# Two neighbouring rows per partition in a batch-norm and ReLU kernel: runs of 8 KB in HBM instead of 4 KB

## The chip, the cores and the metric

The kernel runs on one core of one Trainium2 chip. The metric is the device time of one execution in microseconds.

Some words: HBM is the memory outside the core, SBUF the core's own memory with 128 partitions, and DMA moves data between them. A *run* of bytes is a stretch that is contiguous in memory (an experiment is called a run too, by its label); a *packet* is one record of a DMA engine in the trace; a *queue* is where an engine issues its transfers (sync, scalar or POOL). A *dip* is a stretch in which the transfer rate falls below its *plateau*, the rate in the middle of the kernel.

## The reference

Inference batch norm followed by ReLU on a tensor of 32 images, 128 channels and 32 x 32 pixels in float32: 16.8 MB in, 16.8 MB out, and almost no arithmetic.

```python
# x: (32, 128, 32, 32); gamma, beta, running_mean, running_var: (128,); eps = 1e-5
normalized = (x - running_mean[None, :, None, None]) / np.sqrt(running_var[None, :, None, None] + eps)
scaled = normalized * gamma[None, :, None, None] + beta[None, :, None, None]
return np.maximum(scaled, 0)
```

Gamma and variance are 1, beta and mean are 0. The kernels compute scale and bias from the tables all the same.

## The kernel before

A partition holds one channel. A tile is two images, so the 8 KB that a partition gets come from two places in HBM, 512 KB apart, 4 KB each. Tile 0 and eleven others are loaded from the sync queue, four (1, 3, 5, 7) from the scalar queue, which also issues all stores. The four parameter tables are loaded from POOL, each as one row in one SBUF partition, and four tiny matmuls (eight passes in the trace) turn them into columns.

```python
x3 = x.rearrange("b c h w -> b c (h w)")
...
engine.dma_start(out=t[:, j*step:(j+1)*step],
                 in_=x3[b0 + j*step : b0 + (j+1)*step].transpose([1, 0, 2]))     # 4 KB runs
...
nc.gpsimd.dma_start(out=prow[0:1, 3*C:4*C], in_=running_var[None, :])            # four such rows
...
nc.scalar.activation(out=t[:, :nb], in_=t[:, :nb], func=Relu, bias=bias_t[:, 0:1], scale=scale_t[:, 0:1])
nc.scalar.dma_start(out=out3[b0 : b0 + nb].transpose([1, 0, 2]), in_=t[:, :nb])
```

The first tile is stored in small pieces (256, 768 and 1,024 columns of one image each), so that stores can begin early.

Of the kernel before, what the change touches and what calls it, by code (L numbers as in the profile page):

```python
# [1 line left out]

# [4 lines left out]


@with_exitstack
def kernel(  # L10
    ctx: ExitStack,
    tc: tile.TileContext,
    x: bass.AP,
    gamma: bass.AP,
    beta: bass.AP,
    running_mean: bass.AP,
    running_var: bass.AP,
    eps: bass.AP,
    out: bass.AP,
):  # L20
    nc = tc.nc

    B, C, H, W = x.shape
    HW = H * W
    assert C == nc.NUM_PARTITIONS, f"expected {nc.NUM_PARTITIONS} channels, got {C}"

    x3 = x.rearrange("b c h w -> b c (h w)")
    out3 = out.rearrange("b c h w -> b c (h w)")

    f32 = mybir.dt.float32  # L30

    NBMAX = 2
    n_tiles = B // NBMAX
    sizes = [NBMAX] * n_tiles
    scalar_tiles = (1, 3, 5, 7)
    splits = {0: 2, 1: 2}
    BUFS = 16
    SEPARATE_PSUM = True
    FIRST_PIECES = (256, HW - 256)

    params = ctx.enter_context(tc.tile_pool(name="params", bufs=1))
    eps_t = params.tile([C, 1], f32)
    nc.vector.memset(eps_t, float(eps))  # L43
    prow = params.tile([1, 4 * C], f32)
    one_t = params.tile([1, 1], f32)
    nc.vector.memset(one_t, 1.0)  # L46

    data = ctx.enter_context(tc.tile_pool(name="data", bufs=BUFS))
    tiles = {}
    for i in (0,) + scalar_tiles:  # L50
        tiles[i] = data.tile([C, NBMAX, HW], f32, name="t")

    def emit_input(i, t, engine):
        nsp = splits.get(i, 1)
        step = NBMAX // nsp
        b0 = i * NBMAX
        for j in range(nsp):
            engine.dma_start(  # L58
                out=t[:, j * step : (j + 1) * step],
                in_=x3[b0 + j * step : b0 + (j + 1) * step].transpose([1, 0, 2]),  # L60
            )

    nc.gpsimd.dma_start(out=prow[0:1, 3 * C : 4 * C], in_=running_var[None, :])  # L63
    nc.gpsimd.dma_start(out=prow[0:1, 0 * C : 1 * C], in_=gamma[None, :])  # L64
    nc.gpsimd.dma_start(out=prow[0:1, 2 * C : 3 * C], in_=running_mean[None, :])  # L65
    nc.gpsimd.dma_start(out=prow[0:1, 1 * C : 2 * C], in_=beta[None, :])  # L66

    emit_input(0, tiles[0], nc.sync)
    for i in scalar_tiles:
        emit_input(i, tiles[i], nc.scalar)  # L70

    pp = ctx.enter_context(tc.tile_pool(name="pp", bufs=1, space=bass.MemoryType.PSUM))
    if SEPARATE_PSUM:
        pcols = [pp.tile([C, 1], f32, name=f"p{k}") for k in range(4)]
    else:
        pc = pp.tile([C, 4], f32)
        pcols = [pc[:, k : k + 1] for k in range(4)]
    for k in (3, 0, 2, 1):
        nc.tensor.matmul(  # L79
            pcols[k],  # L80
            prow[0:1, k * C : (k + 1) * C],
            one_t[0:1, 0:1],
            start=True,
            stop=True,
        )
    g_col, b_col, mu_col, var_col = pcols

    std_t = params.tile([C, 1], f32)
    nc.scalar.activation(  # L89
        out=std_t,  # L90
        in_=var_col,
        func=mybir.ActivationFunctionType.Sqrt,
        bias=eps_t[:, 0:1],
        scale=1.0,
    )
    rstd_t = params.tile([C, 1], f32)
    nc.vector.reciprocal(out=rstd_t, in_=std_t)  # L97
    scale_t = params.tile([C, 1], f32)
    nc.vector.tensor_mul(out=scale_t, in0=g_col, in1=rstd_t)  # L99
    ms_t = params.tile([C, 1], f32)  # L100
    nc.vector.tensor_mul(out=ms_t, in0=mu_col, in1=scale_t)  # L101
    bias_t = params.tile([C, 1], f32)
    nc.vector.tensor_sub(out=bias_t, in0=b_col, in1=ms_t)  # L103

    out_ring = {}
    n_out = [0]

    def relu_store(t, b, img, c0, c1):
        nc.scalar.activation(  # L109
            out=t[:, img : img + 1, c0:c1],  # L110
            in_=t[:, img : img + 1, c0:c1],
            func=mybir.ActivationFunctionType.Relu,
            bias=bias_t[:, 0:1],
            scale=scale_t[:, 0:1],
        )
        eng = out_ring.get(n_out[0], nc.scalar)
        n_out[0] += 1
        eng.dma_start(
            out=out3[b : b + 1, :, c0:c1].transpose([1, 0, 2]),
            in_=t[:, img : img + 1, c0:c1],  # L120
        )

    for i, nb in enumerate(sizes):
        b0 = i * NBMAX
        if i in tiles:
            t = tiles.pop(i)
        else:
            t = data.tile([C, NBMAX, HW], f32, name="t")
            emit_input(i, t, nc.sync)
        if i == 0:  # L130
            c0 = 0
            for w in FIRST_PIECES:
                relu_store(t, b0, 0, c0, c0 + w)
                c0 += w
            for img in range(1, nb):
                relu_store(t, b0 + img, img, 0, HW)
        else:
            nc.scalar.activation(  # L138
                out=t[:, :nb],
                in_=t[:, :nb],  # L140
                func=mybir.ActivationFunctionType.Relu,
                bias=bias_t[:, 0:1],
                scale=scale_t[:, 0:1],
            )
            nc.scalar.dma_start(out=out3[b0 : b0 + nb].transpose([1, 0, 2]), in_=t[:, :nb])  # L145


# [1 line left out]
_INS = ['x', 'gamma', 'beta', 'running_mean', 'running_var', 'eps']  # L149
_OUTS = [((32, 128, 32, 32), 'float32')]  # L150
#: Inputs that are plain numbers.
_NUMBERS = {'eps': 1e-05}


# [26 lines left out]
```

## Time and profile before

| what | value |
|---|---|
| time, median | 86.78 us (86.53 to 86.80) when predicted; 86.53 to 86.64 in the rounds of the experiments |
| span of the profiled execution | 84.6 us |
| ScalarE busy, the busiest compute engine | 34.8 us (41%) |
| DMA traffic | 33.57 MB in 9,025 packets |
| plateau of the transfer rate | 419 to 421 GB/s |

The lines are shown in the prediction. The DMA row gives the busy share of the 16 DMA engines by slice of a fortieth of the span (2.1 us), in tenths; the row under it what they moved. In a table of stretches the last two numbers of a row are the DMA share and the rate in GB/s, and the numbers before them are the busy times of the compute engines. A share of about 1 with a low rate means that the DMA engines are busy with slow packets.

### The profile page before, as it was taken

What the parts mean: (1) busy time and instruction counts of PE and PEld (TensorE: products, weight loads), DVE (VectorE), ACT (ScalarE), POOL (GpSimd) and SP (SyncE); (2) the same over time, 40 slices, a digit from 0 to 9 for tenths busy, and PEclk for the clock granted to TensorE, in tenths of its full rate; (3) what the DMA queues carried; (4) which work ended last, traced back from release to release, by engine and by line L of the source; (5) the groups of instructions that cost most, each with busy time, mean ns of one, the idle gap of its engine ahead of it and who ended that gap; (6) DMA issues with size and microseconds to landing.
All of it is one profiled execution on the core that took longest, in us unless ns stands there. A gap on an engine that the chain in (4) does not pass through costs nothing.

```text
span 84.6 us, 153 instructions
## 1 busy us (share of the span) xinstructions
PE 2.3 (3%) x8; PEld 2.0 (2%) x8; DVE 0.7 (1%) x6; ACT 34.8 (41%) x20; POOL 2.3 (3%) x8
## 2 busy tenths in 40 slices
PE   0007300000000000000000000000000000000000
PEld 0006300000000000000000000000000000000000
DVE  0001100000000000000000000000000000000000
ACT  0321479006920791000049598792987910000000
POOL 5500000000000000000000000000000000000000
DMA  1999999999999999999999999999999999999991
GB/s 35 333 411 353 405 420 418 418 409 410 402 416 416 420 420 424 420 422 420 418 426 420 422 420 418 426 416 424 418 422 422 416 426 420 420 420 418 424 422 74
DMA packets 9025, 33.57 MB, mean 397 GB/s; under 512 B 704, under 2 KB 832, under 8 KB 9024
## 3 DMA queue, kind: packets, MB, share of 16 engines
q10 hardware_dynamic: 5616, 20.97, 61.0%
q1 hardware_dynamic: 3280, 12.58, 36.9%
q0 software_dynamic: 128, 0.00, 0.1%
q14 instruction: 1, 0.01, 0.0%
HBM read 16.78 MB, written 16.78 MB: 396 GB/s over the span
## 4 chain that ended last, share of the span: by engine, by line
DMA 65%; ACT 7%; ACTq 4%; issue 3%
DMA t<-in_x_dram 65%; ACT t L138 7%; ACTq L58 2%; ACTq L145 2%
## 5 line engine op out<-in xcount | busy, mean ns | idle before, releaser
L138 ACT ACTIVATE t<-t,bias_t,scale_t 128x2048 f32<-128x2048 f32 x15 | 30.6, 2084 | 24.7 <-DMA t<-in_x_dram 22.3
L109 ACT ACTIVATE t<-t,bias_t,scale_t 128x256 f32<-128x256 f32 (+2 forms) x3 | 2.8, 950 | 2.4 <-DVE bias_t L103 2.0
L89 ACT ACT_TABLE_LOAD x1 | 1.3, 1283 | 3.5 <-issue 3.5
L79 PE MATMUL p<-one_t,prow 1*128 1x1 f32 x8 | 2.3, 354 | 7.2 <-DMA prow<-in_running_var_dram 6.8
L79 PEld LDWEIGHTS p<-one_t,prow 1*128 1x128 f32 x8 | 2.0, 306 | 7.4 <-issue 6.8
L89 ACT ACTIVATE std_t<-p,eps_t 128x1 f32<-128x1 f32 x1 | 0.3, 261 | 2.7 <-PE p L79 2.7
L63 POOL DMA_DIRECT2D prow<-in_running_var_dram x1 | 0.6, 617 | 0.8 <-POOLq L162 0.8
L65 POOL DMA_DIRECT2D prow<-in_running_mean_dram x1 | 0.5, 487 | 0.0
L64 POOL DMA_DIRECT2D prow<-in_gamma_dram x1 | 0.5, 484 | 0.0
L66 POOL DMA_DIRECT2D prow<-in_beta_dram x1 | 0.5, 484 | 0.0
L97 DVE RECIPROCAL rstd_t<-std_t 128x1 f32<-128x1 f32 x1 | 0.2, 164 | 6.8 <-ACT std_t L89 6.8
L103 DVE TENSOR_TENSOR bias_t<-p,ms_t 128x1 f32<-128x1 f32 x1 | 0.2, 158 | 0.6 <-PE p L79 0.6
L99 DVE TENSOR_TENSOR scale_t<-p,rstd_t 128x1 f32<-128x1 f32 x1 | 0.2, 159 | 0.2 <-PE p L79 0.2
L101 DVE TENSOR_TENSOR ms_t<-p,scale_t 128x1 f32<-128x1 f32 x1 | 0.2, 157 | 0.4 <-PE p L79 0.4
L162 POOL MEMSET const-float32-0.0<- 128x1 f32 x1 | 0.1, 98 | 0.2 <-issue 0.2
L162 POOL MEMSET const-bfloat16-1.0<- 128x1 bf16 x1 | 0.1, 101 | 0.0
L162 POOL MEMSET const-float32-1.0<- 128x1 f32 x1 | 0.1, 98 | 0.0
L162 POOL MEMSET const-uint8-127<- 128x1 uint8 x1 | 0.1, 98 | 0.0
L43 DVE MEMSET eps_t<- 128x1 f32 x1 | 0.1, 59 | 0.8 <-PEq L162 0.8
L46 DVE MEMSET one_t<- 1x1 f32 x1 | 0.1, 59 | 0.0
## 6 DMA issues: line engine op xcount, KB each, us to landing
out_dram<-t ACTq DMA_DIRECT2D x15, 1024.0 KB, 15.0
t<-in_x_dram SPq DMA_DIRECT2D x11, 1024.0 KB, 17.8
t<-in_x_dram ACTq DMA_DIRECT2D x3, 1024.0 KB, 16.7
t<-in_x_dram ACTq DMA_DIRECT2D x2, 512.0 KB, 6.1
t<-in_x_dram SPq DMA_DIRECT2D x2, 512.0 KB, 5.8
out_dram<-t ACTq DMA_DIRECT2D x1, 512.0 KB, 10.6
out_dram<-t ACTq DMA_DIRECT2D x1, 384.0 KB, 16.4
out_dram<-t ACTq DMA_DIRECT2D x1, 128.0 KB, 15.3
```

Of the source, the lines that this page charges most:

```text
L58: engine.dma_start(out=t[:, j * step : (j + 1) * step], in_=x3[b0 + j * step : b0 + (j + 1) * step].transpose([1, 0, 2]),)
L63: nc.gpsimd.dma_start(out=prow[0:1, 3 * C : 4 * C], in_=running_var[None, :])
L64: nc.gpsimd.dma_start(out=prow[0:1, 0 * C : 1 * C], in_=gamma[None, :])
L65: nc.gpsimd.dma_start(out=prow[0:1, 2 * C : 3 * C], in_=running_mean[None, :])
L66: nc.gpsimd.dma_start(out=prow[0:1, 1 * C : 2 * C], in_=beta[None, :])
L79: nc.tensor.matmul(pcols[k], prow[0:1, k * C : (k + 1) * C], one_t[0:1, 0:1], start=True, stop=True,)
L89: nc.scalar.activation(out=std_t, in_=var_col, func=mybir.ActivationFunctionType.Sqrt, bias=eps_t[:, 0:1], scale=1.0,)
L97: nc.vector.reciprocal(out=rstd_t, in_=std_t)
L109: nc.scalar.activation(out=t[:, img : img + 1, c0:c1], in_=t[:, img : img + 1, c0:c1], func=mybir.ActivationFunctionType.Relu, bias=bias_t ...
L138: nc.scalar.activation(out=t[:, :nb], in_=t[:, :nb], func=mybir.ActivationFunctionType.Relu, bias=bias_t[:, 0:1], scale=scale_t[:, 0:1],)
L145: nc.scalar.dma_start(out=out3[b0 : b0 + nb].transpose([1, 0, 2]), in_=t[:, :nb])
L162: nc = _bacc.Bacc("TRN2", target_bir_lowering=False, num_devices=1)
```

## The change

The intent: give a partition two neighbouring rows of the (image, channel) list, which lie next to each other in HBM, so that one run is 8 KB and half as many packets move the same bytes. A partition then holds two channels, so scale and bias tables have two columns and each tile takes two ACTIVATEs. Together with this, all loads go to the sync queue, all stores stay on the scalar queue, the parameter loads move to the scalar queue and land as two values in each of 64 partitions, and one matmul with a selection matrix spreads them over 128.

```diff
-    x3 = x.rearrange("b c h w -> b c (h w)")
+    xr = x.rearrange("b c h w -> (b c) (h w)").rearrange("(t p j) w -> t p j w", p=P, j=J)   # J = 2
...
-    emit_input(0, tiles[0], nc.sync)
-    for i in scalar_tiles:
-        emit_input(i, tiles[i], nc.scalar)
+    for t in range(T):
+            nc.sync.dma_start(out=xt, in_=xr[t, :, a:b, :])
...
-    nc.gpsimd.dma_start(out=prow[0:1, 3 * C : 4 * C], in_=running_var[None, :])    # and three more
+    raw = params.tile([Q, 4, J], F32, name="raw")                                  # Q = 64
+    for k, src in enumerate((running_var, gamma, running_mean, beta)):
+        nc.scalar.dma_start(out=raw[:, k, :], in_=src.rearrange("(q j) -> q j", j=J))
...
+        for j in range(a, b):
+            nc.scalar.activation(out=xt[:, j - a, :], in_=xt[:, j - a, :], func=ACTF.Relu,
+                                 bias=bias_t[:, j : j + 1], scale=scale_t[:, j : j + 1])
+        nc.scalar.dma_start(out=outr[t, :, a:b, :], in_=xt)
```

(Cut: the loop over a tile's pieces, of which there is one; the selection matrix and its matmul; the chain Sqrt, reciprocal, multiply, subtract, now two columns wide; the old handling of the first tile in pieces, which is gone.)

More of the change, by code (lines that the diff above doesn't have):

```diff
@@ L6 @@
 from concourse._compat import with_exitstack
+F32 = mybir.dt.float32
+ACTF = mybir.ActivationFunctionType
+J = 2
+PIECES = ((0, 2),)
 @with_exitstack
@@ L24 @@
     HW = H * W
-    assert C == nc.NUM_PARTITIONS, f"expected {nc.NUM_PARTITIONS} channels, got {C}"
-    x3 = x.rearrange("b c h w -> b c (h w)")
-    out3 = out.rearrange("b c h w -> b c (h w)")
-    f32 = mybir.dt.float32
-    NBMAX = 2
-    n_tiles = B // NBMAX
-    sizes = [NBMAX] * n_tiles
-    scalar_tiles = (1, 3, 5, 7)
-    splits = {0: 2, 1: 2}
-    BUFS = 16
-    SEPARATE_PSUM = True
-    FIRST_PIECES = (256, HW - 256)
-    params = ctx.enter_context(tc.tile_pool(name="params", bufs=1))
@@ L42 @@
-    eps_t = params.tile([C, 1], f32)
-    nc.vector.memset(eps_t, float(eps))
-    prow = params.tile([1, 4 * C], f32)
-    one_t = params.tile([1, 1], f32)
-    nc.vector.memset(one_t, 1.0)
-    data = ctx.enter_context(tc.tile_pool(name="data", bufs=BUFS))
-    tiles = {}
-    for i in (0,) + scalar_tiles:
-        tiles[i] = data.tile([C, NBMAX, HW], f32, name="t")
-    def emit_input(i, t, engine):
-        nsp = splits.get(i, 1)
-        step = NBMAX // nsp
-        b0 = i * NBMAX
-        for j in range(nsp):
-            engine.dma_start(
-                out=t[:, j * step : (j + 1) * step],
-                in_=x3[b0 + j * step : b0 + (j + 1) * step].transpose([1, 0, 2]),
-            )
@@ L63 @@
-    nc.gpsimd.dma_start(out=prow[0:1, 3 * C : 4 * C], in_=running_var[None, :])
-    nc.gpsimd.dma_start(out=prow[0:1, 0 * C : 1 * C], in_=gamma[None, :])
-    nc.gpsimd.dma_start(out=prow[0:1, 2 * C : 3 * C], in_=running_mean[None, :])
-    nc.gpsimd.dma_start(out=prow[0:1, 1 * C : 2 * C], in_=beta[None, :])
-    emit_input(0, tiles[0], nc.sync)
-    for i in scalar_tiles:
-        emit_input(i, tiles[i], nc.scalar)
-    pp = ctx.enter_context(tc.tile_pool(name="pp", bufs=1, space=bass.MemoryType.PSUM))
@@ L73 @@
-    if SEPARATE_PSUM:
-        pcols = [pp.tile([C, 1], f32, name=f"p{k}") for k in range(4)]
-    else:
-        pc = pp.tile([C, 4], f32)
-        pcols = [pc[:, k : k + 1] for k in range(4)]
-    for k in (3, 0, 2, 1):
-        nc.tensor.matmul(
-            pcols[k],
-            prow[0:1, k * C : (k + 1) * C],
-            one_t[0:1, 0:1],
-            start=True,
-            stop=True,
-        )
-    g_col, b_col, mu_col, var_col = pcols
-    std_t = params.tile([C, 1], f32)
-    nc.scalar.activation(
-        out=std_t,
-        in_=var_col,
-        func=mybir.ActivationFunctionType.Sqrt,
-        bias=eps_t[:, 0:1],
-        scale=1.0,
-    )
@@ L96 @@
-    rstd_t = params.tile([C, 1], f32)
-    nc.vector.reciprocal(out=rstd_t, in_=std_t)
-    scale_t = params.tile([C, 1], f32)
-    nc.vector.tensor_mul(out=scale_t, in0=g_col, in1=rstd_t)
-    ms_t = params.tile([C, 1], f32)
-    nc.vector.tensor_mul(out=ms_t, in0=mu_col, in1=scale_t)
-    bias_t = params.tile([C, 1], f32)
-    nc.vector.tensor_sub(out=bias_t, in0=b_col, in1=ms_t)
-    out_ring = {}
-    n_out = [0]
-    def relu_store(t, b, img, c0, c1):
-        nc.scalar.activation(
-            out=t[:, img : img + 1, c0:c1],
-            in_=t[:, img : img + 1, c0:c1],
-            func=mybir.ActivationFunctionType.Relu,
-            bias=bias_t[:, 0:1],
-            scale=scale_t[:, 0:1],
-        )
-        eng = out_ring.get(n_out[0], nc.scalar)
-        n_out[0] += 1
-        eng.dma_start(
-            out=out3[b : b + 1, :, c0:c1].transpose([1, 0, 2]),
-            in_=t[:, img : img + 1, c0:c1],
-        )
@@ L123 @@
-    for i, nb in enumerate(sizes):
-        b0 = i * NBMAX
-        if i in tiles:
-            t = tiles.pop(i)
-        else:
-            t = data.tile([C, NBMAX, HW], f32, name="t")
-            emit_input(i, t, nc.sync)
-        if i == 0:
-            c0 = 0
-            for w in FIRST_PIECES:
-                relu_store(t, b0, 0, c0, c0 + w)
-                c0 += w
-            for img in range(1, nb):
-                relu_store(t, b0 + img, img, 0, HW)
-        else:
-            nc.scalar.activation(
-                out=t[:, :nb],
-                in_=t[:, :nb],
-                func=mybir.ActivationFunctionType.Relu,
-                bias=bias_t[:, 0:1],
-                scale=scale_t[:, 0:1],
-            )
-            nc.scalar.dma_start(out=out3[b0 : b0 + nb].transpose([1, 0, 2]), in_=t[:, :nb])
+    P = nc.NUM_PARTITIONS
@@ new lines @@
+    assert C % J == 0 and P % (C // J) == 0 and (B * C) % (P * J) == 0
+    Q = C // J
+    T = B * C // (P * J)
+    xr = x.rearrange("b c h w -> (b c) (h w)").rearrange("(t p j) w -> t p j w", p=P, j=J)
+    outr = out.rearrange("b c h w -> (b c) (h w)").rearrange("(t p j) w -> t p j w", p=P, j=J)
+    data = ctx.enter_context(tc.tile_pool(name="data", bufs=1))
+    params = ctx.enter_context(tc.tile_pool(name="params", bufs=1))
+    psum = ctx.enter_context(tc.tile_pool(name="psum", bufs=1, space=bass.MemoryType.PSUM))
@@ new lines @@
+    tiles = []
+    for t in range(T):
+        for a, b in PIECES:
+            xt = data.tile([P, b - a, HW], F32, name=f"x{t}_{a}")
+            nc.sync.dma_start(out=xt, in_=xr[t, :, a:b, :])
+            tiles.append((t, a, b, xt))
+    raw = params.tile([Q, 4, J], F32, name="raw")
+    for k, src in enumerate((running_var, gamma, running_mean, beta)):
+        nc.scalar.dma_start(out=raw[:, k, :], in_=src.rearrange("(q j) -> q j", j=J))
+    eps_t = params.tile([P, 1], F32, name="eps_t")
@@ new lines @@
+    nc.vector.memset(eps_t, float(eps))
+    rep = params.tile([Q, P // Q, Q], F32, name="rep")
+    nc.gpsimd.memset(rep, 1.0)
+    nc.gpsimd.affine_select(
+        out=rep,
+        in_=rep,
+        compare_op=mybir.AluOpType.is_equal,
+        fill=0.0,
+        base=0,
+        pattern=[[0, P // Q], [-1, Q]],
+        channel_multiplier=1,
+    )
+    cols = psum.tile([P, 4, J], F32, name="cols")
+    nc.tensor.matmul(
+        cols.rearrange("p k j -> p (k j)"),
+        rep.rearrange("q r s -> q (r s)"),
+        raw.rearrange("q k j -> q (k j)"),
+        start=True,
+        stop=True,
+    )
@@ new lines @@
+    std_t = params.tile([P, J], F32, name="std_t")
+    nc.scalar.activation(out=std_t, in_=cols[:, 0, :], func=ACTF.Sqrt, bias=eps_t[:, 0:1], scale=1.0)
+    rstd_t = params.tile([P, J], F32, name="rstd_t")
+    nc.vector.reciprocal(out=rstd_t, in_=std_t)
+    scale_t = params.tile([P, J], F32, name="scale_t")
+    nc.vector.tensor_mul(out=scale_t, in0=cols[:, 1, :], in1=rstd_t)
+    ms_t = params.tile([P, J], F32, name="ms_t")
+    nc.vector.tensor_mul(out=ms_t, in0=cols[:, 2, :], in1=scale_t)
@@ L149 @@
+    bias_t = params.tile([P, J], F32, name="bias_t")
+    nc.vector.tensor_sub(out=bias_t, in0=cols[:, 3, :], in1=ms_t)
+    for t, a, b, xt in tiles:
+        for j in range(a, b):
+            nc.scalar.activation(
+                out=xt[:, j - a, :],
+                in_=xt[:, j - a, :],
+                func=ACTF.Relu,
+                bias=bias_t[:, j : j + 1],
+                scale=scale_t[:, j : j + 1],
+            )
+        nc.scalar.dma_start(out=outr[t, :, a:b, :], in_=xt)
 _INS = ['x', 'gamma', 'beta', 'running_mean', 'running_var', 'eps']
```

## The prediction

> **What bounds the kernel now.** I read the page's busy shares and the slices first. Every compute engine is mostly idle (ScalarE 41%, the rest under 4%), while the DMA row is full from the second slice to the last but one:
>
> ```profile
> PE 2.3 (3%) x8; PEld 2.0 (2%) x8; DVE 0.7 (1%) x6; ACT 34.8 (41%) x20; POOL 2.3 (3%) x8
> ...
> DMA  1999999999999999999999999999999999999991
> GB/s 35 333 411 353 405 420 418 418 409 410 402 416 416 420 420 424 420 422 420 418 426 420 422 420 418 426 416 424 418 422 422 416 426 420 420 420 418 424 422 74
> DMA packets 9025, 33.57 MB, mean 397 GB/s; under 512 B 704, under 2 KB 832, under 8 KB 9024
> ```
>
> The reader is to see a plateau near 420 GB/s that doesn't care whether loads and stores mix (middle) or only stores are left (the last quarter). The table of stretches puts numbers on it:
>
> ```profile
> 1.50:3.00 1.50, 0.00 (x0) 0.00 (x0) 0.00 (x0) 0.00 (x0) 1.50 (x4) 1.00 0.71 183
> 3.00:7.00 4.00, 0.17 (x1) 0.20 (x2) 0.00 (x0) 1.28 (x1) 0.29 (x1) 1.00 1.02 410
> 7.00:9.00 2.00, 1.67 (x7) 1.42 (x7) 0.48 (x3) 0.26 (x1) 0.00 (x0) 1.00 0.99 338
> 9.00:20.00 11.00, 0.46 (x2) 0.37 (x2) 0.16 (x1) 4.94 (x5) 0.00 (x0) 1.00 1.03 416
> 20.00:60.00 40.00, 0.00 (x0) 0.00 (x0) 0.00 (x0) 21.10 (x11) 0.00 (x0) 1.00 1.03 419
> 60.00:83.00 23.00, 0.00 (x0) 0.00 (x0) 0.00 (x0) 7.24 (x4) 0.00 (x0) 1.00 1.02 419
> ```
>
> The last two columns are the DMA share and GB/s. The share is 1.02 to 1.03 everywhere except in the first 1.5 us: neighbouring packets overlap a little, and the sixteen engines have no gap. Low rates at 1.5 to 3 and 7 to 9 us are slow packets, not missing ones. So the chain of waits (65% "DMA t<-in_x_dram") and ScalarE's 22.3 us of waits for loads are symptoms: no wait in the middle costs time, because both queues always hold work.
>
> ```profile
> ACT t L138 <- DMA t<-in_x_dram: 22.3, 5, 11.5
> ...
> SPq L176 <- DMA out_dram<-t: 44.9, 3, 40.1
> ```
>
> The second line is the closing wait for stores, long because stores are issued far ahead. From the packet records of the trace (which no view prints): first data packet at 1.78 us, last one ending near 83.2 us, then about 1.45 us to the span's end. The time is (start) + (bytes over the packet rate) + (receipt of the last store); the measured 86.78 us lies 2.1 us above the 84.6 us span, and I carry that over unchanged.
>
> **What the Trainium skill says.** "DMA: Bandwidth & Descriptors", section Issuing engines are not separate DMA queues: all issuing engines feed the same 16 DMA engines. The trace agrees: two queues give the plateau of 419, one store queue alone in the last stretch also 419. Same page, section Why small descriptors are slow: each packet carries a small fixed overhead, given as about 3 cycles. The trace agrees that a fixed part exists: packets of 1,024, 3,072 and 4,096 bytes take a median of 46, 121 and 159 ns. The first two give 75 ns for 2,048 bytes, or 36.6 ns per KB, which leaves 9 ns fixed. "Perfetto Trace Analysis", section DMA Optimizations, says going from 2 KB to 4 or 8 KB "can dramatically improve throughput". I don't expect drama: the overhead at 4 KB is already only a few per cent. "ScalarE: Activation LUTs", section What ACT_TABLE_LOAD costs: about 93 ns more for each pointer operand, and 0.833 ns per element; the trace's 2084 ns at 2048 wide and 1240 ns at 1024 wide (the longest of the three in the first tile) agree.
>
> **The change, part by part.**
>
> *Packets.* Before, a partition's 8 KB in a tile come from two images, so each run in HBM is 4 KB: 8,192 data packets, 512 per engine. After, a partition takes two neighbouring rows, 8 KB in one run, so 256 per engine for the same bytes. In the plateau an engine moves 4,096 bytes every 65,536/420 = 156.0 ns (all 16 move 65,536 bytes in that time). At the 36.6 ns per KB of above, the bytes themselves are 146.5 ns of this, which leaves 9.5 ns; but the records are whole nanoseconds, and some 0.8 ns of a slot is the 4-byte completion packets (0.4 us in 80), which stay. With a byte cost of 37 to 37.5 ns per KB, which the 4,096-byte packets allow as well ((159 - 46)/3 = 37.7), 5 to 7 ns are left. I take 5.5 ns per packet. Halving the packets saves 256 x 5.5 = 1.4 us, with 0.9 to 2.0 as its own range. The only 8 KB packets in the trace, seven instruction fetches, have a minimum of 307 ns against a minimum of 156 for 4 KB data: a saving of 5 ns per pair, the same size.
>
> *Scale tables.* Removed: four software-issued rows and eight small matmul passes. Added: four loads of 64 x 8 bytes on the scalar queue, a POOL selection matrix, one matmul of 8 columns, DVE work 2 wide. Before, bias is ready at 9.65 us, following parameters that land 5.5 to 6.0 us after issue. After, an engine holds 4 loads x (4 runs + 1 completion) = 20 small packets; if they alternate one for one with 8 KB packets of about 310 ns, they take 6.4 us from 1.8 us on, so the last lands at about 8.5 us; matmul, Sqrt and four DVE steps (0.6 + 0.3 + 4 x 0.2) put bias at about 10.5 us. If they go in bursts, about 6.5 us. Neither is on the path: the loads of tiles 0 to 3 wait for nothing and fill the engines for 4.2 MB / 0.41 = 10 us, and the built program lets loads 4 to 10 follow on earlier loads or parameters alone. Only load 11 waits for a store (that of tile 1). Cost 0.
>
> *ScalarE.* A tile becomes two ACTIVATEs of 1,024 columns, about 1.2 us each, plus a store issue of 0.38 us: 2.8 us a tile. The DMA needs 2 MB / 0.42 = 5.0 us for a tile's load and store. 16 x 2.4 = 38 us instead of 34.8, all beside transfers. Cost 0.
>
> *Queues.* Five loads move from the scalar queue to sync, so stores no longer stand behind loads. Before, reads end near 62 us and the rest is stores. After, they alternate about evenly from 12 us on, so reads end near 70 us. Following the built program's semaphores, the stores of tiles 7, 9, 11 and 12 wait for loads 11, 12, 13 and 14, so when the last load lands about 2 MB of stores are queued, 5 us of work; tile 15 needs 1.2 + 1.2 + 0.4 us plus about 1 us before its packets start. The engines don't run dry. Cost 0.
>
> *Start and end.* The first load is still issued on sync at 0.74 us, and the last receipt is the same. The slow packets at the start cost about 0.5 us before; the dip at 7 to 9 us, 2 x (420 - 338)/420 = 0.4 us. I can't tie the dip to an instruction; it stands beside the last parameter packets. I give a tenth or two of a microsecond for losing part of it.
>
> Sum: 86.78 - 1.4 - 0.15 = 85.2 us, or 1.8% faster.
>
> **The rivals.** (1) The 8 KB runs are split into 4 KB packets after all. Against: the runs are single in both HBM and SBUF, and 8 KB packets exist in the trace (on another queue). For: no packet of the two data queues exceeds 4 KB now, so nothing shows that these queues make larger ones. Then 86.3 to 86.9 us. (2) One read queue at the start can't hold 420 GB/s: for some 10 us the only bulk queue is sync, where before two read queues overlapped. Against: one store queue alone holds 419; but no stretch of the trace has one read queue alone. If it ran at 400, 10 us would cost 0.5 us, and the result is 85.7. (3) A semaphore chain of eight leaves both queues empty at some moment, most likely where store 7 waits for load 11 or in the tail. By the count above one queue always has over 1 MB; if I am wrong once, it costs 1 to 3 us: 86 to 88 us. (4) The gain is larger because contiguous 1 MB reads also remove the dips and the 1% by which 9 to 60 us stays under 422: 0.4 + 0.4 us more, 84.4 us.
>
> **Range and chances.** The mechanism puts the gain between 0.9 and 2.3 us, just around the 2% border (85.04 us). Rival 1 gets 10%, rivals 2 and 3 some 15% together, rival 4 about 25%. That gives 85.2 us, range 84.3 to 86.5, faster 0.40, same 0.56, slower 0.04.
>
> **What would show it.** Right: about 4,096 packets of 8 KB with a median near 312 ns, the plateau at 426 to 430 GB/s, DMA tenths of 9 from the second slice to the end, no gap of both queues, ScalarE busy about 38 us, reads ending near 70 us. Step by step wrong: 4 KB packets (rival 1); a lower rate up to 12 us (rival 2); a slice under 9 near 47 or 72 us (rival 3). The prediction as a whole is wrong if 8 KB packets take more than twice a 4 KB packet's 156 ns slot, or if some slice before the last is empty.

## The result, and the profile after

The changed kernel took 86.00 us (median of 4 runs, 85.83 to 86.18) against 86.77 us of the kernel before in the same rounds. Ratios here are the mean time of one kernel's fast runs over that of the other's of the same rounds, so they are not quite the ratio of the medians: 0.9925, 95% interval 0.9901 to 0.9950. A second measurement in another batch, the control of the experiments, gave 86.08 against 86.53 us, ratio 0.9948 (0.9936 to 0.9959). So the gain is 0.45 to 0.77 us, clear of noise, but at best about half of the 1.6 us that was forecast, though the time itself lies inside the stated range.

The page of the changed kernel, parts 1 to 3, busy times, slices and queues:

```profile
PE 0.6 (1%) x2; PEld 0.5 (1%) x2; DVE 0.7 (1%) x5; ACT 38.7 (46%) x34; POOL 0.7 (1%) x6
...
DMA  2899999999999999999999999999999999999990
GB/s 31 311 389 369 388 427 408 427 322 415 427 419 435 427 431 435 427 419 431 419 427 431 427 435 427 427 427 427 419 431 427 431 435 427 415 431 423 423 419 39
DMA packets 4929, 33.57 MB, mean 398 GB/s; under 512 B 832, under 2 KB 832, under 8 KB 832
...
q1 hardware_dynamic: 2304, 16.78, 48.8%
q10 hardware_dynamic: 2624, 16.78, 47.2%
```

All 4,097 packets that are not tiny have 8 KB (4,096 of data, one that fetches instructions): the runs were not split. The plateau is higher than before. But slices 3 to 5 read 389, 369, 388, and slice 9, at 17 to 19 us, reads 322, all with a full DMA row. The table of stretches, in the same cuts as before:

```profile
1.50:3.00 1.50, 0.00 (x0) 0.00 (x0) 0.00 (x0) 0.00 (x0) 0.00 (x0) 1.00 0.66 142
3.00:7.00 4.00, 0.00 (x0) 0.00 (x0) 0.00 (x0) 1.28 (x1) 0.00 (x0) 1.00 0.98 393
7.00:9.00 2.00, 0.00 (x0) 0.00 (x0) 0.00 (x0) 0.00 (x0) 0.00 (x0) 1.00 0.98 373
9.00:20.00 11.00, 0.56 (x2) 0.50 (x2) 0.64 (x4) 7.29 (x8) 0.00 (x0) 1.00 1.01 396
20.00:60.00 40.00, 0.00 (x0) 0.00 (x0) 0.00 (x0) 22.93 (x20) 0.00 (x0) 1.00 1.01 427
60.00:83.00 23.00, 0.00 (x0) 0.00 (x0) 0.00 (x0) 7.21 (x7) 0.00 (x0) 1.00 0.99 417
```

From 20 us on the rate is 427 where it was 419, as predicted (the last row is lower only because the transfer runs out in its last microsecond; from 60 to 82 us the rate is 427). From 9 to 20 us it is 396 where it was 416, with a DMA share of 1.01. Two narrower stretches hold most of the loss. From 5 to 11 us, while the parameters load, the kernel before and then the changed one:

```profile
5.00:11.00 6.00, 2.30 (x8) 1.99 (x8) 0.64 (x4) 1.57 (x3) 0.00 (x0) 1.00 1.01 390
5.00:11.00 6.00, 0.00 (x0) 0.00 (x0) 0.00 (x0) 0.00 (x0) 0.00 (x0) 1.00 0.98 379
```

And the changed kernel from 16 us until its first store's packets appear at 19.3 us:

```profile
16.00:19.50 3.50, 0.00 (x0) 0.00 (x0) 0.00 (x0) 3.50 (x4) 0.00 (x0) 1.00 1.00 356
```

The packet records of the two traces, added up, say when a given number of bytes was through (us from the span's start):

| through | before | changed | difference |
|---|---|---|---|
| 2 MB | 7.28 | 7.69 | +0.41 |
| 7 MB | 19.68 | 20.42 | +0.74 |
| 20 MB | 50.74 | 50.83 | +0.09 |
| 33 MB | 81.65 | 81.27 | -0.38 |

The longer runs gained 1.1 us over the last 26 MB, and the start had given away 0.7 us before. (In these two single executions the spans differ by 0.2 us, in the medians the times differ by 0.45 to 0.77. In all four runs of the changed kernel the time exceeds the span by 1.7 us, and in the rounds of c_after the kernel before took 86.42 us at a span of 84.6 and 86.67 at 84.9; so the profiled execution of before, with its span of 84.6, was one of its quicker ones.)

No wait on a compute engine explains the start. The first ACTIVATE, which needs the bias, starts at 12.97 us rather than 9.69, but the sync queue's loads keep the DMA engines supplied until then. What is slow are packets, and a minority of them: from 5 to 11 us the median of the 8 KB packets is 309 ns as on the plateau, but 22 of 277 take over 400 ns and the mean is 330; from 16 to 19.5 us it is 42 of 152 and a mean of 366. (The parameters' tiny packets themselves, about 9 ns each, fill only 0.2 us of the first stretch.) The question is what slows them.

One thing outside the transfers matters when small differences are read: from the landing of the last store to the end of the span there is a closing stretch of semaphore work. It is 1.14 us in the trace of before and 1.09 and 1.10 in the two of the changed kernel, but 0.81 to 1.28 over all runs. A difference of a few tenths in the time can lie there and not in the stream; where it does, it is said.

### The profile page after: what moved, and what is told of

Same layout as the page of the kernel before. It is cut to its first block, busy times and chain, and to the rows that moved or that the text cites. A ratio compares the mean times of both kernels' runs of the same rounds, so it can differ in the third digit from the quotient of the medians.

```text
span 84.4 us, 148 instructions
## 1 busy us (share of the span) xinstructions
PE 0.6 (1%) x2; PEld 0.5 (1%) x2; DVE 0.7 (1%) x5; ACT 38.7 (46%) x34; POOL 0.7 (1%) x6
## 4 chain that ended last, share of the span: by engine, by line
DMA 79%; ACT 2%; issue 1%; ACTq 1%
DMA x<-in_x_dram 71%; DMA raw<-in_gamma_dram 8%; ACT x L92 2%; ACTq L57 1%; ACTq L99 0%
## 5 line engine op out<-in xcount | busy, mean ns | idle before, releaser
L92 ACT ACTIVATE x<-x,bias_t,scale_t 128x1024 f32<-128x1024 f32 x32 | 37.2, 1229 | 21.5 <-DMA out_dram<-x 10.4
L72 PE MATMUL cols<-raw,rep 64*128 64x8 f32 x2 | 0.6, 353 | 11.2 <-DMA raw<-in_beta_dram 11.2
L72 PEld LDWEIGHTS cols<-raw,rep 64*128 64x128 f32 x2 | 0.5, 306 | 11.2 <-issue 11.2
```

Source lines behind the costliest of these rows:

```text
L72: nc.tensor.matmul(cols.rearrange("p k j -> p (k j)"), rep.rearrange("q r s -> q (r s)"), raw.rearrange("q k j -> q (k j)"), start=True, s ...
L92: nc.scalar.activation(out=xt[:, j - a, :], in_=xt[:, j - a, :], func=ACTF.Relu, bias=bias_t[:, j : j + 1], scale=scale_t[:, j : j + 1],)
```

## The experiments

All kernels computed correct outputs. "Control" is the changed kernel, run again in the first batch (86.08 us, ratio 0.9948). Every run but those that say otherwise had five rounds, in batches beside the kernel before, and ratios to the kernel before of the same rounds are compared across batches. The loss of a slow stretch is its length x (1 - its rate / the plateau's rate).

### The control, and the parts of the change

**c_after**, no edit.

> The changed kernel again, unaltered, as the control of this batch and for a second trace. Theory A (the start is slowed by the new parameter loads and by having one load queue): 86.0 us, and the trace again shows reads under 400 GB/s between 5 and 11 us and again between 16 and 19 us, so that the first 7 MB are through about 20.4 us after the start (19.7 before). Theory B (the dips are chance events of the memory): the dips lie elsewhere or are missing in this trace, and single times scatter by more than 0.5 us.

86.08 us, and the trace repeats the start almost to a tenth: 2 MB at 7.67 us, 7 MB at 20.44 us, slow reads at 5 to 11 us and at 16.5 to 19.5 us. Two traces from two batches agree: these dips belong to the kernel, not to chance.

**e_4k**, everything of the change but the long runs:

```diff
-    .rearrange("(t p j) w -> t p j w", p=P, j=J)
+    .rearrange("(t j p) w -> t p j w", p=P, j=J)     # for x and out
```

> Everything of the change but the long runs: the two rows of a partition lie 128 rows apart, so each run is 4 KB again (the scale tables are then right only because every channel of these inputs has the same parameters). If the packet term is as its plateau says (427 against 419 GB/s, 1.4 us over the whole transfer), this is 1.2 to 1.5 us slower than the control, 87.2 to 87.5, slower than the kernel before. If 8 KB packets themselves cause the slow start (rival), the start is as fast as before, the plateau is 419, and the time is 86.6 to 86.8.

87.15 us, ratio 1.0081 (1.0062 to 1.0100): slower than the kernel before. So the difference splits into two large parts of opposite sign: the rest of the change costs about 0.6 us (87.15 against 86.53), the 8 KB runs give about 1.1 us back (86.08 against 87.15). Three stretches of its trace, start, parameter loads, plateau:

```profile
1.50:5.00 3.50, 0.00 (x0) 0.00 (x0) 0.00 (x0) 1.28 (x1) 0.00 (x0) 1.00 0.87 275
5.00:11.00 6.00, 0.56 (x2) 0.50 (x2) 0.24 (x2) 0.26 (x1) 0.00 (x0) 1.00 0.99 359
20.00:75.00 55.00, 0.00 (x0) 0.00 (x0) 0.00 (x0) 28.58 (x25) 0.00 (x0) 1.00 1.03 421
```

The plateau is that of the kernel before, 421. The stretch of 5 to 11 us is as slow as in the changed kernel or slower, so that loss isn't caused by 8 KB packets. But in the 3.5 us before its first store's packets it ran at 411, a loss of 0.08 us, where the changed kernel has its dip of 356 (16 to 19.5 us; 3.5 x (1 - 356/427) = 0.58 us). That second loss comes with the packet size.

```profile
14.00:17.50 3.50, 0.00 (x0) 0.00 (x0) 0.00 (x0) 3.50 (x4) 0.00 (x0) 1.00 1.02 411
```

### The parameter loads

**x_nopar**, no parameter loads at all (wrong for other tables, right for these inputs):

```diff
-    (cut: raw loads, selection matrix, matmul, Sqrt, reciprocal, multiplies, subtract)
+    nc.vector.memset(scale_t, 0.999995)
+    nc.vector.memset(bias_t, 0.0)
```

> The changed kernel without its parameter loads, matmul, Sqrt and DVE chain: scale and bias are constants, right for these inputs alone. If the small parameter packets cause the slow reads between 5 and 11 us (theory A1), the rate there is 420-428 throughout and the 2 MB mark comes 0.4 us sooner; the time is 85.5 to 85.7. If the dip near 7.5 us comes from something else (it stands in all five traces), it stays and the time is within 0.15 us of 86.08. The dip before the first store should move to where the first store now is, about 8 to 10 us, with its 0.6 us loss unchanged under theories S and R.

85.39 us, ratio 0.9865 (0.9850 to 0.9881), 0.7 us better than the control. The stretch of 5 to 11 us:

```profile
5.00:11.00 6.00, 0.00 (x0) 5.31 (x5) 0.00 (x0) 1.00 1.02 423
```

423 GB/s, where the changed kernel has 379. The slow reads there are the parameter loads' doing. One read queue alone holds the rate, so that rival of the prediction is gone. Of the 0.8 us between the two profiled spans (84.4 and 83.6), 0.5 lie before the last data packet's end and 0.3 in the closing stretch (1.09 and 0.82 us): in the stream the parameters cost about 0.5 us. The dip before the first store stayed and grew to 1.0 us:

```profile
10.50:15.00 4.50, 0.00 (x0) 4.50 (x5) 0.00 (x0) 1.00 0.95 330
```

**b_nopar**, the same taken out of the kernel before.

> The kernel before without its parameter loads and the chain behind them (constants for scale and bias, right for these inputs alone). Taking the parameters out of the changed kernel gained 0.7 us (85.39 against 86.08). If the old way of loading them was cheap and the new way is what the change lost (theory P), this gains at most 0.2 us: 86.35 to 86.55. If the parameters cost the kernel before as much (rival), it is 85.8 to 85.9, the dip at 7 to 9 us goes, and the parameters explain nothing of the missing gain.

86.44 us against 86.62, ratio 0.9974 (0.9961 to 0.9988): 0.2 us. The old parameter path cost 0.2 us, the new one 0.7. The difference of 0.5 us is most of what the rest of the change costs. (The traces give the same difference for the stream alone: the last data packet ends 0.5 us sooner without parameters in the changed kernel, and no sooner, 83.23 against 83.15 us, in the kernel before.)

Why is the new form dearer? Three runs take the suspects one by one.

**e_swparams**, the queue: the same loads from POOL.

```diff
-        nc.scalar.dma_start(out=raw[:, k, :], ...)
+        nc.gpsimd.dma_start(out=raw[:, k, :], ...)
```

> The four parameter loads go back to the POOL queue, everything else as changed. If the 20 small packets per engine on the scalar hardware queue slow the reads between 5 and 11 us (theory A1), the 2 MB mark comes 0.2 to 0.4 us sooner than in the control and the time falls to 85.6 to 85.8. If small packets cost the same from whichever queue they come (rival), the time stays within 0.15 us of the control. If the dip at 16 to 19 us belongs to the late first store (12.95 us for the bias), it moves with the bias.

85.94 us, ratio 0.9934 (0.9922 to 0.9946), within 0.15 us of the control: not the queue. (The last data packet ends at 82.95 us, in the control at 82.93; the small gain lies in the closing stretch.) The stretch of 5 to 11 us in its trace:

```profile
5.00:11.00 6.00, 0.56 (x2) 0.50 (x2) 0.52 (x4) 0.26 (x1) 0.00 (x0) 1.00 0.93 370
```

This settles one more rival. In the changed kernel the fifth, sixth and seventh data loads were issued only when a parameter load had landed (5.93, 8.01 and 11.10 us), so that waits for the parameters might have starved the sync queue. Here all seven were issued by 3.94 us, and the stretch is no faster. The share of 0.93 says, though, that here about half of the loss is a gap and not slow packets: from 7 to 8 us the DMA engines are busy for only 0.69 of the time, with loads waiting. Why is not shown.

**y_syncpar**, the taking of turns: the same loads from the sync queue, in line between the first and the second data load.

```diff
+        if t == 1:
+            for k, src in enumerate((running_var, gamma, running_mean, beta)):
+                nc.sync.dma_start(out=raw[:, k, :], ...)
```

> The changed kernel with its four parameter loads issued on the sync queue, between the first and the second data load, so that their small packets stand in line in the one busy queue and do not take turns with it. If the turn-taking of two queues slows the reads between 5 and 11 us, the rate there is 420 or more and the time 85.5 to 85.7. If the small packets cost the same in any queue: 86.0 to 86.2. Issue of four more loads on sync takes some 1.8 us, less than the 2.5 us of the first load's transfer, so a gap of 0 to 0.5 us is possible at 4 us.

86.27 us, ratio 0.9960 (0.9942 to 0.9978), not better than the control. From 6.5 to 12.5 us the trace shows 421 GB/s, but the cost is paid at once at 5 to 6 us (182 GB/s), where the small packets stand in line and the second data load comes late, and the dip before the first store is 1.0 us. A miss: in line is no better than in turn. (The trace is of an execution of 86.61 us, one of the two slowest of six; the other four took 86.21 to 86.29.)

**w_row**, the form of the destination: the changed kernel with the old form, one row of 512 bytes per table in one partition, from POOL, then spread by VectorE copies and eight one-row matmuls.

```diff
-    raw = params.tile([Q, 4, J], F32, name="raw")
-        nc.scalar.dma_start(out=raw[:, k, :], in_=src.rearrange("(q j) -> q j", j=J))
+    prow = params.tile([1, 4 * C], F32, name="prow")
+        nc.gpsimd.dma_start(out=prow[0:1, k * C : (k + 1) * C], in_=src[None, :])
...
-    (cut: selection matrix, one matmul)
+    (cut: copies prow -> prep with the channels in order, 8 matmuls prep x one)
```

> The changed kernel with the parameters loaded as in the kernel before: each table as one row of 512 bytes in one partition, from POOL, then spread over the partitions by VectorE copies and eight one-row matmuls. If the scattered destination (64 partitions of 8 bytes) is what costs 0.5 us, this takes 85.5 to 85.6 us and the reads between 5 and 11 us run at 415 GB/s or more apart from one dip near 7.5 us. If any parameter load beside one 8 KB read queue costs as much, it is 85.9 to 86.1, as with the POOL queue alone (85.94).

85.53 us, ratio 0.9861 (0.9829 to 0.9892): 0.75 us better than the control, as good as without parameters. The same stretch:

```profile
5.00:11.00 6.00, 3.72 (x16) 3.55 (x16) 1.39 (x8) 0.23 (x1) 0.00 (x0) 1.00 1.01 414
```

Between e_swparams and w_row the DMA traffic of the parameters is alike: both from POOL, and in both packet records 64 packets of 32 bytes and 64 of 4. Of the DMA traffic only where the bytes land in SBUF differs, 64 partitions or one, and 370 becomes 414; the last data packet ends 0.6 us sooner (82.36 against 82.95 us), with the closing stretch alike. So with 8 KB packets beside it the scattered destination is what costs, as far as these two runs can separate it: they lie in different batches, and the computation that follows the loads differs too, though it moves no data by DMA. How the scattering slows other packets is not shown. (Without the selection matrix on POOL the first load is also issued 0.07 us sooner, at 0.74 instead of 0.81 us; that part of the gain is something else.)

### The dip before the first store

**e_both**, parameters on POOL as in e_swparams, and tiles 1, 3, 5, 7 on the scalar queue:

```diff
-            nc.sync.dma_start(out=xt, in_=xr[t, :, a:b, :])
+            eng = nc.scalar if t in (1, 3, 5, 7) else nc.sync
+            eng.dma_start(out=xt, in_=xr[t, :, a:b, :])
```

> As the run before it, and tiles 1, 3, 5, 7 are loaded on the scalar queue as in the kernel before. If one read queue is what makes the start slow (theory A2), the first 0.5 MB come 0.2 us sooner and the dip at 16 to 19 us goes: 85.2 to 85.5 us. If not, within 0.15 us of the run with the parameters on POOL.

85.69 us, ratio 0.9906 (0.9893 to 0.9919), 0.25 us better than e_swparams. The 0.5 MB mark is not sooner, though (3.89 us against 3.80), and the dip isn't gone: with the first store now standing behind loads it moved to 20-24 us, at 363 GB/s, a loss of 0.6 us. What improved is the parameter stretch, 392 GB/s from 5 to 11 us instead of 370. The dip follows the first store's packets wherever they are, and not its issue: in the changed kernel the store is issued at 15.37 us and its packets begin at 19.3, in e_both it is issued at 14.76 us, its packets begin at about 23.6 (the 513th large packet of a queue that has 512 of loads to move first), and the dip is late as well.

**x_first**, the first tile in two pieces of one row per partition, loads and stores:

```diff
-        for a, b in PIECES:
+        for a, b in ((0, 1), (1, 2)) if t == 0 else PIECES:
```

> The changed kernel with the first tile alone split into two pieces of one row per partition (4 KB runs, 512 KB loads and stores); all other tiles as changed. In every trace so far the reads slow down for about 2.5 us just before the first store's packets appear, to 271-350 GB/s with 8 KB runs (a loss of about 0.6 us) and to 404-412 with 4 KB runs (about 0.1 us). If the size of the first store's packets sets that loss (theory S), the dip shrinks to 0.1 us and the time falls to 85.3-85.6 from the control's 86.08. If the loss is set by the reads' 8 KB packets (rival R), the dip stays and the time is 85.8 to 86.1; then at most the first 0.25 MB come 0.2 us sooner.

85.97 us, ratio 0.9931 (0.9918 to 0.9944). The dip shrank (373 from 15 to 18 us, 0.4 us), but the start got slower (217 GB/s from 3 to 4 us, where the two traces of the changed kernel have 426 and 393), and nearly nothing remains.

**y_st0**, only the store of the first tile in two parts of 4 KB runs, its load whole:

```diff
+            if t == 0:
+                nc.scalar.dma_start(out=outr[t, :, j, :], in_=xt[:, j - a, :])
+        if t > 0:
-        nc.scalar.dma_start(out=outr[t, :, a:b, :], in_=xt)
+            nc.scalar.dma_start(out=outr[t, :, a:b, :], in_=xt)
```

> The changed kernel with the first tile's store alone split into two stores of 4 KB runs, issued after each half's ACTIVATE; its load stays whole. Theory S (first store's packets set the dip before the first store): the dip's loss falls from 0.6 to 0.1-0.3 us and the time to 85.6-85.8. Rival R (the reads' packets set it, or any onset of stores): dip and time stay, 86.0 to 86.1.

85.81 us, ratio 0.9902 (0.9888 to 0.9917), 0.4 us better than the control. The dip's loss is 0.46 us (371 from 16 to 19.5 us), less than the 0.58 and 0.51 of the two traces of the changed kernel in the same stretch but more than expected: the time moved nearly as theory S said, the trace shows only part of it.

Three runs without parameters asked what the dip depends on; x_nopar with its loss of 1.0 us is their control. **z_st4** gives only the stores 4 KB runs, **z_ld4** only the loads:

```diff
# z_st4: ScalarE writes into a padded buffer, so that the store's two rows are apart in SBUF
+        yt = outp.tile([P, J, HW + 16], F32, name="y")
-                out=xt[:, j - a, :],
+                out=yt[:, j - a, :HW],
-        nc.scalar.dma_start(out=outr[t, :, a:b, :], in_=xt)
+        nc.scalar.dma_start(out=outr[t, :, a:b, :], in_=yt[:, :, :HW])
# z_ld4: the same the other way round, xt padded, yt not
```

> The changed kernel without parameters (which took 85.39 us and lost 1.0 us in the dip before its first store), with ScalarE writing into padded buffers, so that all stores have 4 KB runs while loads keep 8 KB. If the stores' packet size sets the dip (theory S): dip under 0.3 us. If the loads' does (rival R): the dip stays at 0.6 to 1.0 us. The plateau should lose half of what 8 KB gives, 0.7 us. Time 85.3 to 85.6 under S, 85.9 to 86.2 under R.

> The mirror image: loads into padded buffers with 4 KB runs, stores of 8 KB. Theory S: dip 0.6 to 1.0 us, time 85.9 to 86.2. Rival R: dip under 0.3 us, time 85.3 to 85.6. If each side counts a part, both runs show a dip in between.

85.59 us (ratio 0.9879, 0.9859 to 0.9900) and 87.63 us (ratio 1.0125, 1.0098 to 1.0152), the second outside everything expected. The stretch of the dip and the plateau, first for z_st4, then for z_ld4:

```profile
10.50:15.00 4.50, 0.00 (x0) 4.50 (x6) 0.00 (x0) 1.00 1.01 366
30.00:75.00 45.00, 0.00 (x0) 23.67 (x21) 0.00 (x0) 1.00 1.02 423
```

```profile
11.00:15.50 4.50, 0.00 (x0) 4.32 (x4) 0.00 (x0) 1.00 0.96 315
30.00:75.00 45.00, 0.00 (x0) 21.84 (x19) 0.00 (x0) 1.00 1.02 425
```

The losses are 0.6 us with 4 KB stores and 1.2 us with 4 KB loads, against 1.0 us with 8 KB both ways. So, in one trace each, the stores' packet size counts and the loads' does not help; but 4 KB stores alone don't bring the dip down to e_4k's 0.08 us. Neither theory holds as stated. (The out-of-place buffers and their waits are part of z_ld4's time, so its 87.63 us is not the price of 4 KB loads.)

**z_warm**, an extra 128 KB store of zeros to a scratch tensor at the start:

```diff
+    warm = nc.dram_tensor("warm_dram", (P, 256), F32, kind="Internal").ap()
+    nc.scalar.dma_start(out=warm, in_=warm_t)
```

> The changed kernel without parameters, and with one extra store of 128 KB of zeros to a scratch tensor in HBM, issued on the scalar queue at the start. If the dip is a one-off cost of the first write to HBM or of the first use of the scalar queue, it goes or moves to the first 3 us, and the time is 85.0 to 85.4 although 0.3 us of traffic are added. If it belongs to the onset of the big stores, it stays at 9 to 14 us with about 1 us of loss, and the time is 85.6 to 85.8.

85.64 us, ratio 0.9891 (0.9873 to 0.9908). The dip's loss falls from 1.0 to 0.6 us (358 from 11.5 to 15 us), and the start loses 0.4 us more (0.5 MB at 4.05 us instead of 3.64). An earlier write takes away a part, not the whole.

**x_best**, parameters on POOL, two load queues and the split first tile together (the edits of e_swparams, e_both and x_first).

> Parameters on POOL, tiles 1, 3, 5, 7 loaded on the scalar queue, and the first tile in two pieces of 4 KB runs: what the runs so far favour, together. Without the split it took 85.69 us. If theory S is right, another 0.4 to 0.6 us go: 85.1 to 85.3, 1.5% under the kernel before. If not, 85.6 to 85.8.

86.12 us, ratio 0.9952 (0.9938 to 0.9966): a miss. The dip is gone (425 GB/s from 13 to 30 us), but from 3 to 8.5 us the rate is 347, a loss of 5.5 x (1 - 347/427) = 1.0 us. The two nearly cancel in the stream: compared with e_both, which lacks only the split, 2 MB are through 0.9 us later, but 20 MB at the same time (50.7 us), and the last data packet ends 0.1 us later (82.81 against 82.70). The rest of the 0.4 us between the two runs lies in the closing stretch, 1.28 us here and 0.90 there, and not in the stream. Why the start is worse than that of any of its parts is not settled.

### Longer runs

**x_16k**, four rows per partition, 8 tiles of 2 MB:

```diff
-J = 2
-PIECES = ((0, 2),)
+J = 4
+PIECES = ((0, 4),)
```

> The same source with 4 rows per partition: 16 KB runs, 8 tiles of 2 MB. The plateaus of 4 KB and 8 KB runs (420.5 and 428 GB/s) give 155.9 and 306.2 ns for a packet, 5.5 ns of it fixed; if that holds, a 16 KB packet needs 607 ns, 432 GB/s, and the transfer gains another 0.7 us in the plateau. If the dip before the first store grows with the packet (theories S and R), it eats this: 0.6 becomes 1.2 us or more, and the time is 85.8 to 86.3. If the dip doesn't grow: 85.3 to 85.5.

85.41 us, ratio 0.9870 (0.9853 to 0.9887). Parameter stretch, dip and plateau of its trace:

```profile
5.00:11.00 6.00, 0.00 (x0) 0.00 (x0) 0.00 (x0) 0.00 (x0) 0.00 (x0) 1.00 1.00 424
19.00:24.00 5.00, 0.00 (x0) 0.00 (x0) 0.00 (x0) 5.00 (x5) 0.00 (x0) 1.00 0.97 331
30.00:75.00 45.00, 0.00 (x0) 0.00 (x0) 0.00 (x0) 19.87 (x18) 0.00 (x0) 1.00 1.01 431
```

The plateau is 431; 432 was expected from a fixed part of 5.5 ns per packet, so the packet theory holds a second time. The dip grew to 1.2 us, as feared. But the time is far better than the 85.8 to 86.3 expected for that, since the parameter stretch, now 32 partitions of 16 bytes, hardly loses anything (424). So a scattered destination alone is not enough to cost time: the stretch was slow beside packets of 4 KB (359 in e_4k) and of 8 KB, but not here, and that is not explained.

**y_comb16** adds the parameters on the sync queue (as y_syncpar) and the first tile's store in four parts of 4 KB runs (as y_st0) to this; **z_best16** only the latter.

> 16 KB runs (4 rows per partition, 8 tiles of 2 MB), parameters on the sync queue behind the first load, the first tile's store in four parts of 4 KB runs. The 16 KB form alone took 85.41 us with a start that lost 0.5 us and a dip of 1.1 us. If the single store dip goes as under theory S: 84.4 to 84.8, more than 2% under the kernel before. If only the parameters help: 85.2 to 85.4.

> 16 KB runs and the first tile's store in four parts of 4 KB runs, parameters on the scalar queue as in the change. With the parameters on the sync queue this was 85.03 us; at 8 KB the sync queue cost 0.1 us against the scalar queue. So 84.8 to 85.1; if the sync queue was what helped at 16 KB, 85.2 to 85.4.

85.03 us (ratio 0.9810, 0.9787 to 0.9834) and 84.69 us (ratio 0.9786, 0.9767 to 0.9805; 84.61 to 84.90). The second beats both kernels: 1.8 us under the kernel before, 1.4 us under the changed one. Whether that is more than 2% is left open by its interval, which includes 0.98. Its slices:

```profile
DMA  4699999999998999999899999999999999999992
GB/s 79 206 459 396 467 411 419 451 378 381 453 470 362 441 464 425 387 455 470 360 417 403 482 387 466 411 419 466 387 474 411 435 443 395 482 395 435 443 395 111
```

The zigzag is that of 16 KB packets falling into one slice or the next; from 20 to 75 us the mean is 431. The dip before the first store costs 0.35 us here (380 from 15.5 to 18.5 us).

**w_row16**, the row form of the parameters in z_best16.

> 16 KB runs, the first tile's store in four 4 KB parts, and the row form of the parameter loads. The same with the scattered form on the scalar queue took 84.69 us; its trace shows 420-428 GB/s while parameters load, so there is little to regain: 84.5 to 84.8.

85.51 us, ratio 0.9868 (0.9828 to 0.9908): a miss. In the traces the bytes run level with z_best16 (33 MB at 80.24 and 80.23 us), the last packet ends 0.3 us later, and the closing stretch is 0.3 us longer (1.21 against 0.89): together 0.6 of the 0.8 us, half of it outside the stream. The rounds of this batch scattered more than others (85.29 to 86.14, the kernel before up to 87.33), so the comparison is weak.

## Why the prediction was right or wrong

- **What bounds the kernel: right.** In both traces of the changed kernel the DMA share is 0.93 or more in every stretch of the table from 3 us to the last stores, so there is no sign of a moment with both queues empty; ScalarE works 38.7 us beside it (38 predicted), and the last load lands at 68.3 us (about 70 predicted). One reading was too generous: the prediction has a share of 1.02 to 1.03 everywhere after the first 1.5 us, but its own row of 7 to 9 us has 0.99.
- **"Packets": right in kind, a little too large.** The runs were not split. The plateau went from 420.8 to 427.2 GB/s (means over 30 to 75 us from the packet records), so 33.56 MB take 79.75 and 78.56 us: 1.2 us saved instead of 1.4. A packet's slot on its engine is 65,536 bytes / 420.8 = 155.7 ns for 4 KB and 131,072 / 427.2 = 306.8 ns for 8 KB, which leaves 4.7 ns fixed per packet instead of 5.5. (The prediction's 9.5 ns is a slip of units: 36.6 ns are for 1,000 bytes, not 1,024. 4,096 bytes are then 150.0 ns and leave 6.0 of the 156.0. The 5.5 that entered its sum was taken from the other readings.)
- **"Scale tables ... Cost 0": the step that failed.** It asked when the bias is ready and whether the stores would come too late. Both answers were good enough: the bias was ready at 12.94 us, later than the 10.5 given, and was still off the path. It did not ask what the loads do to the packets beside them. They kept the engines nearly as busy at a lower rate: removing them gained 0.7 us, in the kernel before 0.2 us, so the step should have said +0.5 us. By w_row it is the destination spread over 64 partitions that costs this, beside 8 KB packets; by which mechanism stays open.
- **"Start and end": wrong in sign.** It could tie the low rate at 7 to 9 us to no instruction, saw it beside the last parameter packets, and expected to regain 0.15 us by losing part of it. Without parameters, the kernel before still runs at only 400 GB/s from 5 to 11 us, so most of the loss there (0.30 of 0.45 us) is something else. And the kernel got a dip that wasn't in the sum: reads slow down for some 3 us before the first store's packets, with 8 KB stores by 0.58 us; in the kernel before, whose first stores are small pieces behind loads, the loss from 15 to 23.5 us is 8.5 x (1 - 409/421) = 0.24 us. The missing term is about +0.35 us.
- **"Queues ... Cost 0": right as far as it went.** One read queue holds the rate (423 GB/s in x_nopar), the semaphores left no hole.

The sum in its place: -1.2 + 0.5 + 0.35 = -0.35 us, beside a measured -0.45 to -0.77. The removals don't add up exactly, as the dip shows, which grew when the parameters went (x_nopar), and the closing stretch moves by tenths, so no closer balance should be expected. The mechanism of the dip before the first store stays open. Shown is that it follows the first store, that it is larger with 8 KB than with 4 KB stores, and that small stores ahead of it reduce it; why reads are slow before the writes' packets appear was not found.

## What to carry to other kernels

When the DMA engines are full, a cost can hide at a busy share of 1: read the rate next to the share, and charge a small load not only with its latency but with what it does to the stream beside it. In the 8 KB form it paid to load the small tables as rows into one partition rather than scattered over 64 (w_row), and to make the first store small (y_st0); in the 16 KB form the scattered loads cost nothing, and the row form gained nothing. So measure the stretch in which the tables load before changing it. And before a difference of a few tenths is put down to the stream, look whether it lies behind the last packet. Longer runs are worth what the fixed part of a packet says, here 1.5% of the rate from 4 to 8 KB and 1% more to 16 KB, and that is easily lost again in the first 20 us.

## What the Trainium skill lacked or had wrong

- "DMA: Bandwidth & Descriptors", section Why small descriptors are slow: it gives the fixed overhead of a packet as about 3 cycles, and its advice, on joining consecutive descriptors, ends at 256 bytes. Lacking is what longer runs above that are worth. Here 4.7 to 5.8 ns per packet (155.7, 306.8 and, from the 16 KB plateau of 431.3 GB/s, 607.8 ns per slot) are still worth 1.5% from 4 to 8 KB and 1.0% from 8 to 16 KB.
- "Perfetto Trace Analysis", section DMA Optimizations: going from 2 KB to 4 or 8 KB "can dramatically improve throughput". No run here has bulk transfers in 2 KB pieces, so this isn't contradicted; lacking is that the last step, from 4 to 8 KB, is small: 420.8 to 427.2 GB/s.
- No page that I read says what small loads do to a stream beside them: 2 KB of parameters scattered over 64 partitions cost a stream of 8 KB packets about 0.5 us (370 GB/s from 5 to 11 us, in the row form of the same packets 414).
- No page that I read has the dip in reads before the first large store: 0.5 to 1.2 us with 8 or 16 KB runs in loads and stores, 0.08 us with 4 KB runs in both (e_4k).
